# An adaLN, RG-LRU and attention block: its opening rebuilt around a transposed x and four accumulators, and one pair of merge gates moved

## The chip, the cores and the metric

The kernel runs on one core of one Trainium2 chip. The metric is device time in microseconds, the median of three runs. A core has the engines TensorE (PE), VectorE (DVE), ScalarE (ACT), GpSimd (POOL) and SyncE (SP); each runs its own queue of instructions in order and waits on semaphores for the others. SP mostly starts DMAs; here POOL and ACT start some too.

## The reference, cut to what matters

```python
def reference(x, c, positions, ...):          # B=1, S=1024, D=1024
    mod = c @ w_ada + b_ada                    # shift, scale, gate: 3 x 1024
    shift, scale, gate = split(mod, 3)
    h = rmsnorm(x, norm_g) * (1 + scale) + shift
    z = h @ w_in                               # q, k, v, attention gate, RNN x, RNN gate, two merge gates
    ...
    attn = sliding_window_attention_with_sinks(rope(q), rope(k), v, sinks) * silu(ga)
    rnn  = rg_lru(causal_depthwise_conv(xr), ...) * silu(gr)
    m = sigmoid(ma) * (attn @ w_attn_proj) + sigmoid(mr) * (rnn @ w_rnn_proj)
    out = rmsnorm(x + gate * (m @ w_out), final_g)
```

`rmsnorm` multiplies each token of x by 1/sqrt(mean of its squares + eps) and by the gain.

## The kernel before, in words

Everything is float32 in accuracy: every operand of a main product is split into a high part (a rounding to the matmul's own format, called `hh`, `wh`, `nh`) and a low part (what is left: `hl`, `wl`, `nl`), and each product is three matmuls, high by high, weight-low by high, weight-high by low (`mm_k`, L169). A weight half arrives in a tile `r` (`load_half`), ScalarE casts it (`cast`, L101, with a scale L103) and VectorE subtracts (`rest`, L107, with a scale L109) into one of five slots.

The residual stream is used transposed: `xT[kc]` holds 128 of the 1024 features by all 1024 tokens, in eight pieces kc. The **opening** builds it. SP loads x in 8 tiles of 128 tokens (512 KB each). ScalarE and VectorE take turns at the sums of squares, which run along a tile's row (L310, L312); a root, a reciprocal and a scaling follow for each tile (L317 to L319); TensorE transposes 64 blocks (L324) and ScalarE copies them out (L326). The modulation is worked out on VectorE: for each piece two passes `jk` (L221) multiply rows of `w_ada` (SP, 16 loads of 512 KB) with c, broadcast over the partitions by a matmul at L194, and add up each row; `gsc` (L226) and the addition of a bias (L229) finish it. An affine on VectorE (L345) applies it to the piece, ScalarE casts the high halves (L348, `hha` and `hhb` for the first and second 512 tokens of the first four pieces), VectorE subtracts the low halves (L350, `hla`, `hlb`). TensorE accumulates three chunks of 128 output columns over the pieces, the two of k and one of q (48 matmuls of 512 columns each). The framework orders this part; a few `issue_after` push it. The rotary table (positions times frequencies, reduced to a turn by 29 small operations on VectorE, a sine on ScalarE, four DMAs on POOL's queue) is made in its gaps.

From there on **the program is written in the order in which each engine runs it**. The V product (192 matmuls of 256 columns, L1290 to L1292) and the fourth of the opening's chunks (48) follow, while POOL forms differences of the pieces (L382 to L385, `differences`) and ScalarE and VectorE the operands from them (L390, L391). Then come 23 pairs of chunks. A `Pair` computes two chunks with seven half-size products instead of eight: seven slots of 12 matmuls (`product`, L511). Its results stand in four PSUM banks; the pair's place in the list, odd or even (`par`), chooses which of the banks is its second and which its fourth. Work for ScalarE and VectorE is planned into slots: some steps at fixed ones (`at_slot`), others when there is room (`waiting`, `background`), each with a cost. The last pair has an extra step, an addition of its fourth bank to a kept copy (L582).

Of the pairs the last runs beside the attention (scores L1047, their copy L1055, masking L1061, reduction L1066, weights L1071, transposes L1085, values L1119), which goes on while the projections are worked out (`rp`, through `mm_k` at L169). `rp`'s two accumulators are opened when the pairs are done, in the space of the first to fourth banks: the first in `bk[0]` and `bk[1]`, the second in `bk[2]` and `bk[3]`. In the orders below the four banks are called `bk_68` to `bk_71`.

Of the kernel before, what the change touches and what calls it, by code (L numbers as in the profile page):

```python
# [18 lines left out]
ALU = mybir.AluOpType  # L19
# [32 lines left out]
def tile_hybrid_block(ctx, tc, x, pk, rows, posr, posi, invf, c_row, w_ss, w_gate, w_main, w_v,  # L52
# [103 lines left out]
    hx = h_ctx.enter_context(tc.tile_pool(name="hx", bufs=8))  # L156
    xT = [xx.tile([P, S], F32, name=f"xT{kc}") if kc % 4 == 3 else
# [20 lines left out]

    with ExitStack() as st:
        sp = st.enter_context(tc.tile_pool(name="start", bufs=1, side="right"))  # L180
        posr_t = sp.tile([P, 64], I32, name="posr_t")
        dma(posr_t[:], posr)
        invf_t = sp.tile([P, 1], F32, name="invf_t")
        dma(invf_t[:], invf)
        dma(pk_t[:], pk)
        make_identity(nc, ident)

        c_row_t = sp.tile([1, D], F32, tag="xt", name="c_row_t", bufs=10)
        dma(c_row_t[:], c_row)
        one_row = sp.tile([1, P], F32, name="one_row")  # L190
        V.memset(one_row[:], 1.0)
        c_bc = sp.tile([P, D], F32, name="c_bc")
        for hf in range(2):
            T.matmul(bk[hf], one_row[:], c_row_t[:, SL[hf]], start=True, stop=True)  # L194
            A.copy(c_bc[:, SL[hf]], bk[hf])

        xt = []
        starts = []
        wada = {}

        def load_ss(kc):
            for a in range(2):
                wa_t = sp.tile([P, D], F32, tag="xt", name="wada", bufs=10)
                dma(wa_t[:], w_ss[a * D + kc * P:a * D + (kc + 1) * P, :])
                wada[kc, a] = wa_t

        def load_xt(i):
            t = sp.tile([P, D], F32, tag="xt", name="xt", bufs=10)
            dma(t[:], x[i * P:(i + 1) * P, :])
            xt.append(t)  # L210
# [3 lines left out]
        bsc1 = sp.tile([P, 8], F32, name="bsc1")  # L214
        V.tensor_scalar(out=bsc1[:], in0=pk_t[:, PK_BSC:PK_BSC + 8], scalar1=1.0, scalar2=None,
                        op0=ALU.add)

        def modulate(kc):
            for a in range(2):
                jk = sp.tile([P, D], BF16, tag="junk2", name="jk")  # L220
                V.scalar_tensor_tensor(out=jk[:], in0=wada[kc, a][:], scalar=1.0, in1=c_bc[:],  # L221
                                       op0=ALU.mult, op1=ALU.mult,
                                       accum_out=mods[:, a * 8 + kc:a * 8 + kc + 1])
            shf = mods[:, kc:kc + 1]
            g1 = gsc[:, kc:kc + 1]
            V.scalar_tensor_tensor(out=g1, in0=mods[:, 8 + kc:9 + kc],  # L226
                                   scalar=bsc1[:, kc:kc + 1], in1=pcol(PK_NG, kc),
                                   op0=ALU.add, op1=ALU.mult)
            V.tensor_tensor(out=shf, in0=shf, in1=pcol(PK_BSH, kc), op=ALU.add)  # L229
            return g1, shf  # L230

        def load_start(i):
            w = load_w(w_main[i], 0.125 if i == 2 else 1.0)
            starts.append((w, new_ps() if i < 2 else bk[2:]))

        def tiny(name, n=64):
            return sp.tile([P, n], F32, name=name)

        posf = tiny("posf")
        V.tensor_copy(posf[:], posr_t[:])  # L240
        ang = tiny("ang")
        V.tensor_scalar(out=ang[:], in0=posf[:], scalar1=invf_t[:, 0:1], scalar2=None,
                        op0=ALU.mult)
# [55 lines left out]
        for i in range(8):  # L299
            load_xt(i)  # L300
# [1005 lines left out]
    for i in range(4):  # L1306
        differences(i)
# [364 lines left out]
```

## Time and profile before

| | before |
|---|---|
| time, median of 3 runs | 932.31 us (931.2 to 933.3) |
| profiled execution | 934.7 us, of which the span is 933.0 |
| TensorE busy | 907.5 us, 97% of the span |
| VectorE busy | 687.9 us, 74% |
| ScalarE busy | 533.5 us, 57% |
| GpSimd busy | 108.4 us, 12% |
| first main matmul | 27.84 us |

The profile is of one execution. A row of a timeline reads: start, duration, engine, line, operation, output <- inputs, shape, count, and in brackets how long the engine stood idle before it and what ended that. Durations of operations in a row overlap (an engine starts the next before the last has drained), so what one costs is the distance from one start to the next. A row of the windows reads: the stretch and its length, then for each engine the busy time and the number of instructions, TensorE's granted clock, the DMA's share and GB/s. A group's row gives busy time, mean ns of one, and idle time before.

### The profile page before, as it was taken

The numbers are of one execution on the slowest core, as the hardware profiler recorded it, in microseconds if no ns is written. First come the engines' busy times: TensorE is split into PE (matmuls) and PEld (weight loads), VectorE is DVE, ScalarE is ACT, GpSimd is POOL, SyncE is SP. The second block draws the span as 40 slices with busy tenths as digits, with TensorE's granted clock in tenths as the row PEclk, the third lists the DMA queues.
The fourth block names the chain that finished last, engine by engine and source line by source line (L and its number), as shares of the span: only waits on it lengthen the run. The fifth ranks groups of instructions, "written<-read, shape, count | busy, mean of one in ns | idle before, by whom it ended". The sixth has DMA issues, their size and how long they took to land.

```text
span 933.0 us, 12428 instructions
## 1 busy us (share of the span) xinstructions
PE 907.5 (97%) x4261; PEld 752.7 (81%) x4261; DVE 687.9 (74%) x1068; ACT 533.5 (57%) x1040; POOL 108.4 (12%) x161
## 2 busy tenths in 40 slices
PE   5899999999999999999999998999999999999997
PEld 3689888878888888888887887878888888888886
DVE  8977888877669964996677774899999737657422
ACT  7435565454567656775596783888887632213211
POOL 1047000000000000000000001354454300000000
PEclk9999999999999999999999998999999999999999
DMA  8923587951332541354145347997656186436311
GB/s 324 365 69 125 162 285 228 316 191 48 113 105 98 181 158 37 139 172 149 57 147 180 107 163 257 327 328 222 223 177 193 57 309 228 161 123 238 136 68 67
DMA packets 81140, 164.20 MB, mean 176 GB/s; under 512 B 12771, under 2 KB 29155, under 8 KB 81078
## 3 DMA queue, kind: packets, MB, share of 16 engines
q1 hardware_dynamic: 77734, 155.32, 49.0%
q0 software_dynamic: 2192, 6.00, 1.9%
q10 hardware_dynamic: 1152, 2.10, 0.6%
q8 instruction: 33, 0.54, 0.2%
q14 instruction: 29, 0.24, 0.1%
HBM read 114.00 MB, written 49.78 MB: 176 GB/s over the span
## 4 chain that ended last, share of the span: by engine, by line
PE 87%; DVE 5%; DMA 2%; ACT 2%; issue 1%; SPq 1%; POOL 0%; ACTq 0%; DVEq 0%
PE bk L511 44%; PE rp L169 12%; PE pmain L169 8%; PE rp L1537 5%; PE pgate L799 5%; PE pmain L1537 4%; PE s_ps L1047 3%; PE pv L1119 2%; PE pt L1085 1%; PE bk L169 1%; DMA qs<-q_d 1%; DMA r<-w_rp 1%; SPq L59 1%; DVE wl L107 1%; ACT xT L326 1%
## 5 line engine op out<-in xcount | busy, mean ns | idle before, releaser
L511 PE MATMUL bk<-nh,wl 128*128 128x512 f32 x368 | 144.5, 393 | 0.4 <-DVE wl L107 0.4
L511 PE MATMUL bk<-nh,wh 128*128 128x512 f32 x368 | 144.3, 392 | 0.0
L511 PE MATMUL bk<-nl,wh 128*128 128x512 f32 x368 | 144.0, 391 | 0.0
L107 DVE TENSOR_TENSOR wl<-r,wh 128x512 fp32r<-128x512 f32 x108 | 79.4, 739 | 17.8 <-ACT wh L101 17.8
L101 ACT CAST wh<-r 128x512 fp32r<-128x512 f32 x108 | 66.5, 620 | 34.4 <-DMA r<-w_ap 12.2
L511 PEld LDWEIGHTS bk<-nh,wl 128*128 128x128 f32 x368 | 69.7, 189 | 15.8 <-DVE wl L107 1.4
L511 PEld LDWEIGHTS bk<-nl,wh 128*128 128x128 f32 x368 | 69.6, 189 | 14.5
L511 PEld LDWEIGHTS bk<-nh,wh 128*128 128x128 f32 x368 | 69.7, 189 | 14.3
L511 PE MATMUL bk<-hh,wh 128*128 128x512 f32 x184 | 71.6, 389 | 0.0
L511 PE MATMUL bk<-hh,wl 128*128 128x512 f32 x184 | 71.6, 389 | 0.0
L511 PE MATMUL bk<-hl,wh 128*128 128x512 f32 x184 | 71.6, 389 | 0.0
L107 DVE TENSOR_TENSOR wl<-ws,wh 128x512 fp32r<-128x512 f32 x80 | 54.4, 685 | 1.9 <-ACT wh L101 1.9
L59 POOL DMA_DIRECT2D yh_d<-yh x1 | 0.6, 583 | 471.9 <-ACT yh L866 471.9
L1071 ACT ACTIVATE p<-p,small 128x129 f32<-128x129 f32 x128 | 50.1, 401 | 0.0
L101 ACT CAST wh<-ws 128x512 fp32r<-128x512 f32 x80 | 48.0, 614 | 2.0 <-DVE ws L533 1.1
L1047 PE MATMUL s_ps<-ks,qs 128*128 128x256 f32 (+1 forms) x256 | 38.5, 294 | 2.7 <-DMA qs<-q_d 2.5
L511 PEld LDWEIGHTS bk<-hl,wh 128*128 128x128 f32 x184 | 34.5, 188 | 7.2
L511 PEld LDWEIGHTS bk<-hh,wl 128*128 128x128 f32 x184 | 34.5, 188 | 7.1
L511 PEld LDWEIGHTS bk<-hh,wh 128*128 128x128 f32 x184 | 34.5, 188 | 7.0
L1554 ACT ACTIVATE o<-xo 128x1024 f32<-128x1024 f32 (+2 forms) x10 | 8.9, 889 | 52.9 <-DVE xo L1553 52.9
L614 ACT ACTIVATE c<-bk 128x512 f32<-128x512 f32 x31 | 18.5, 598 | 32.7 <-PE bk L511 32.7
L1047 PEld LDWEIGHTS s_ps<-ks,qs 128*128 128x128 f32 x256 | 33.2, 194 | 3.8 <-issue 2.8
(356 smaller groups left out, 2274.3 us busy)
## 6 DMA issues: line engine op xcount, KB each, us to landing
r<-w_main SPq DMA_DIRECT2D x100, 256.0 KB, 4.2
wada<-w_ss SPq DMA_DIRECT2D x16, 512.0 KB, 9.2
qs<-q_d SPq DMA_DIRECT2D x16, 512.0 KB, 6.0
ks<-k_d SPq DMA_DIRECT2D x24, 192.0 KB, 3.8
xt<-x SPq DMA_DIRECT2D x8, 512.0 KB, 5.7
q_d<-rhi SPq DMA_DIRECT2D x16, 256.0 KB, 3.6
q_d<-rlo SPq DMA_DIRECT2D x16, 256.0 KB, 3.0
wg<-w_gate SPq DMA_DIRECT2D x8, 512.0 KB, 5.5
```

What stands on the lines that cost most here:

```text
L59: return eng.dma_start(dst, src)
L101: A.copy(dst[0][:], src)
L107: V.tensor_tensor(out=dst[1][:], in0=src, in1=f32(dst[0][:]), op=ALU.subtract)
L169: mm = T.matmul(ps[hf], ww, xx[kc][hf], start=(kc == 0 and ww is w_h and xx is xh), stop=(kc == KC - 1 and xx is xl))
L326: A.copy(xT[kc][:, SL[hf]], pt)
L511: W["pe"] = T.matmul(ps, ww[:, c], b[kc][xx_], start=(first and kc == 0 and i == 0), stop=(kc == 3 and i == 2), skip_group_check=not first)
L614: A.activation(t["t"], s(), AF.Tanh, scale=0.5)
L799: W["pe"] = T.matmul(ps[:, SL[hf]], ww[:, c0:c0 + P], xx_[:, SL[hf]], start=(ic == 0 and i == 0), stop=(ic == 1 and i == 2))
L1047: W["pe"] = T.matmul(o, qs[:, j, qc], ks[:, b, k0 + (0 if n else P):k0 + 256], start=(b == 0), stop=(b == 1))
L1071: A.activation(px[:, j, :], px[:, j, :], AF.Exp, bias=sm[:, 0, j:j + 1], accum_out=sm[:, 1, j:j + 1])
L1119: W["pe"] = T.matmul(pv[:], b, m[:].rearrange("p j q -> p (j q)"), start=(i == 0), stop=(i == len(prods) - 1))
L1537: T.matmul(ps[:, sl], lhs[k][th][:, ts_], w[:, sl], start=(k == 0 and w is h_ and lhs is mh), stop=(k == KC - 1 and lhs is ml))
```

## The change

It rebuilds the opening and moves the first pair of merge gates.

- x also comes in transposed (`x_t`), and is loaded straight into `xT`, eight loads at the head of SP's queue. The transposes, their copies and the scaling of tiles are gone (x itself is still read at the end of the kernel).
- The sums of squares now run over partitions: ScalarE squares each piece (L254) into one of four buffers (`acc`, `sqa`, `r_bc`, `sqb`), VectorE adds pieces 0+1, 2+3 and 4+5 (L256), and TensorE sums with 40 matmuls of one moving column (L250), the squares being the weights, into one bank. VectorE reduces (L339, L340), ScalarE takes the root, VectorE the reciprocal (L346), and TensorE spreads the result over the partitions with 8 matmuls (L348). VectorE multiplies the pieces by it (L353 from PSUM, L356 from a copy).
- The modulation rows get their bias as a 1025th column, so two small operations per piece go. ScalarE makes the high halves directly from the normed piece with scale and bias (L359), and applies the affine to the piece (L363).
- The whole opening is in a written order. The angle operations stand first on VectorE; the positions and frequencies are loaded on POOL's queue, c and the constants on ScalarE's.
- Four chunks are accumulated over the pieces, the two of k and both of q. Their first halves of weights have tiles of their own (`first`), the second halves are cast and subtracted at pieces 2 and 3. At pieces 3 to 7 the chunks go in the order 3, 2, 0, 1.
- The differences move from POOL to VectorE (L468 to L471), between the two halves of the V product.
- `MA[0]`, the first pair of merge gates, leaves the list of pairs (23 become 22). Its two chunks are computed as plain products of 48 matmuls (`merge`), one behind the other, directly behind V, with their tanh and stores.
- `gate_row` (the last modulation row, worked out in the background) starts ahead of `v_prep`, in a third waiting list; RNN steps that need its pool wait for it.

The diff, cut to its core:

```diff
-        for kc in range(KC):
-            pt = bk[kc % (2 if hf else 4)]
-            for j in range(4):
-                T.transpose(pt[:, j * P:(j + 1) * P],
-                            xt[hf * 4 + j][:, kc * P:(kc + 1) * P], ident[:])
-            A.copy(xT[kc][:, SL[hf]], pt)
...
+        dma(c_row_t, c_row, A)
+        dma(pk_t[:], pk, A)
+        dma(posr_t[:], posr, G)
+        dma(invf_t[:], invf, G)
...
+        for kc in range(KC):
+            dma(xT[kc][:], x_t[kc * P:(kc + 1) * P, :])
+        load_ss(0)
+        for i in range(4):
+            load_wh(i, 0)
...
+        def sums(i, kc, js=range(8)):
+            for j in js:
+                T.matmul(bk[2][:, 8 * i + j:8 * i + j + 1], sqs[kc % 4][:, j * P:(j + 1) * P],
+                         one[:, 0:1], start=True, stop=True)
+
+        def square(kc):
+            A.activation(sqs[kc % 4][:], xT[kc][:], AF.Square)
+            if kc < 6 and kc % 2:
+                V.tensor_tensor(out=sqs[kc % 4 - 1][:], in0=sqs[kc % 4 - 1][:],
+                                in1=sqs[kc % 4][:], op=ALU.add)
+                sums(kc // 2, kc - 1)
...
+        def spread(hf):
+            r1 = rr[:, 4 * hf:4 * hf + 4]
+            V.reciprocal(r1, r1)
+            for j in range(4):
+                T.matmul(bk[hf][:, j * P:(j + 1) * P], r1[:, j:j + 1].to_broadcast([P, P]),
+                         ident[:], start=True, stop=True)
...
+        def high(kc, hf):
+            A.activation(hh[kc][hf], xT[kc][:, SL[hf]], AF.Identity,
+                         scale=gsc[:, kc:kc + 1], bias=mods[:, kc:kc + 1])
...
+        angles()
+        square(0)
+        square(1)
+        for kc in range(2, 6):
+            square(kc)
+        square(6)
+        sums(3, 6)
+        square(7)
+        for hf in range(2):
+            sums(4, 7, range(4 * hf, 4 * hf + 4))
+        modulate(0, 0)
+        root_of(0)
+        root_of(1)
+        spread(0)
+        spread(1)
...
+        for kc in range(1, KC):
+            norm(kc)
+            for hf in range(2):
+                high(kc, hf)
+            affine(kc)
+            if kc == 1:
+                table()
+            if kc + 1 < KC:
+                for a in range(2):
+                    modulate(kc + 1, a)
+            if kc in (2, 3):
+                for i in (0, 1) if kc == 2 else (2, 3):
+                    cast_w(i, 1)
+                    rest_w(i, 1)
+            low(kc)
...
+            if kc < 3:
+                for terms in ("h", "l"):
+                    for w, ps in starts:
+                        mm_k(ps, w, kc, terms=terms)
+            else:
+                for i in (3, 2, 0, 1):
+                    w, ps = starts[i]
+                    mm_k(ps, w, kc)
...
-    pairs = [Q[1], MA[0], Q[2], MA[1], Q[3], XR[0], GR[0], GA[0], XR[1], GR[1], GA[1], GR[2],
-             XR[2], GA[2], GA[3], GR[3], XR[3], MA[2], MA[3]] + MR
+    pairs = [Q[1], Q[2], MA[1], Q[3], XR[0], GR[0], GA[0], XR[1], GR[1], GA[1], GR[2], XR[2], GA[2],
+             GA[3], GR[3], XR[3], MA[2], MA[3]] + MR
...
+    merge(0, bk[:2])
+    v_store(bk[2:], 1)
...
+    merge(1, bk[2:])
+    merge_out(1, bk[2:])
```

Three places of the new order, each beside the old one. First TensorE at the start of the program, in before from the last transposes to the first main matmuls (`pmain` and `bk_70` are accumulators, `hha_158` the high first half of piece 0):

```order
L324 MATMUL bk_68<-ident,xt 128x128 x3
L324 MATMUL bk_69<-ident,xt 128x128 x3
L324 MATMUL bk_68<-ident,xt 128x128
L324 MATMUL bk_69<-ident,xt 128x128
L324 MATMUL bk_68<-ident,xt 128x128 x4
L324 MATMUL bk_69<-ident,xt 128x128 x4
```

and in the changed kernel from its first instruction to the first main matmuls (`one` is a column of ones, `rr` the reciprocal roots):

```order
L228 MATMUL bk_68<-sqb,one 128x512
L228 MATMUL bk_69<-sqb,one 128x512
L250 MATMUL bk_70<-one,acc 128x1 x8
L250 MATMUL bk_70<-one,r_bc 128x1 x8
L250 MATMUL bk_70<-one,acc 128x1 x8
L250 MATMUL bk_70<-one,r_bc 128x1 x8
L250 MATMUL bk_70<-one,sqb 128x1 x8
L348 MATMUL bk_68<-ident,rr 128x128 x4
L348 MATMUL bk_69<-ident,rr 128x128 x4
L170 MATMUL pmain<-hha_158,wh_203 128x512
```

Transposes gave way to sums and spreading matmuls, in one fixed order. Next VectorE at piece 3, before (`xT_191` is the piece, `hla_172` and `hlb_173` its low halves):

```order
L345 TENSOR_SCALAR xT_191<-xT_191,gsc,mods 128x1024
L221 SCALAR_TENSOR_TENSOR jk,mods<-wada,c_bc 128x1024
L350 TENSOR_TENSOR hla_172<-xT_191,hha_170 128x512
L221 SCALAR_TENSOR_TENSOR jk,mods<-wada,c_bc 128x1024
L350 TENSOR_TENSOR hlb_173<-xT_191,hhb_171 128x512
L229 TENSOR_TENSOR mods<-mods,pk_t 128x1
```

and now (the piece is `xT_193`):

```order
L356 TENSOR_TENSOR xT_193<-xT_193,r_bc 128x1024
L237 SCALAR_TENSOR_TENSOR jk,mods<-wada,c_bc 128x1025 [waits DMAHW2_49]
L237 SCALAR_TENSOR_TENSOR jk,mods<-wada,c_bc 128x1025 [waits DMAHW3_49,DVE_49]
L241 SCALAR_TENSOR_TENSOR gsc<-mods,pk_t 128x1 [waits DVE_49]
L109 SCALAR_TENSOR_TENSOR wl<-r,wh 128x512 [waits DMAHW0_49,Activation_49]
L109 SCALAR_TENSOR_TENSOR wl<-r,wh 128x512 [waits DMAHW1_49,Activation_49]
L368 TENSOR_TENSOR hla_172<-xT_193,hha_170 128x512
L368 TENSOR_TENSOR hlb_173<-xT_193,hhb_171 128x512
```

The low halves of the piece now stand behind both modulation passes of the next piece and two weight subtractions. Last TensorE where the pairs end and `rp` begins, before:

```order
L511 MATMUL bk_70<-nl,wh 128x512
L1119 MATMUL pv<-phc,vs 128x512 [waits DMASW5_49,DVE_49,Activation_49]
L1119 MATMUL pv<-plc,vs 128x512 [waits DVE_49]
L1119 MATMUL pv<-phm,dv 128x512 [waits DMASW4_49,Pool_49]
L1119 MATMUL pv<-plm,dv 128x512 [waits Pool_49]
L1085 MATMUL pt<-ident,p 128x128 [waits PE_49]
L1085 MATMUL pt<-ident,p 128x128 x3
L1047 MATMUL s_ps<-ks,qs 128x256 [waits DMAHW1_49,DMAHW2_49,DMAHW0_49,DVE_49]
L1047 MATMUL s_ps<-ks,qs 128x256 x7
L169 MATMUL rp_5620<-hha_158,wh 128x512 [waits Activation_49]
```

and now:

```order
L597 MATMUL bk_69<-nl,wh 128x512
L1212 MATMUL pv<-phc,vs 128x512 [waits DMASW7_49,DVE_49,Activation_49]
L1212 MATMUL pv<-plc,vs 128x512 [waits DVE_49]
L1212 MATMUL pv<-phm,dv 128x512 [waits DMASW6_49,Pool_49]
L1212 MATMUL pv<-plm,dv 128x512 [waits Pool_49]
L1178 MATMUL pt<-ident,p 128x128 [waits PE_49]
L1178 MATMUL pt<-ident,p 128x128 x3
L1140 MATMUL s_ps<-ks,qs 128x256 [waits DMAHW6_49,DMAHW7_49,DMAHW0_49,DVE_49]
L1140 MATMUL s_ps<-ks,qs 128x256 x7
L170 MATMUL rp_5538<-hha_158,wh 128x512 [waits DVE_49]
```

The last product writes the second bank (`bk_69`) instead of the third (`bk_70`), and the first matmul of `rp` waits for VectorE instead of ScalarE: for the last pair's addition of that bank (L582 before, L668 now).

More of the change, by code (lines that the diff above doesn't have):

```diff
@@ L51, in tile_hybrid_block @@
 @with_exitstack
-def tile_hybrid_block(ctx, tc, x, pk, rows, posr, posi, invf, c_row, w_ss, w_gate, w_main, w_v,
+def tile_hybrid_block(ctx, tc, x, x_t, pk, rows, posr, posi, invf, c_row, w_ss, w_gate, w_main, w_v,
                       w_g, w_ap, w_rp, w_out, out):
@@ L918, in out_row @@
             dma(gate_d, t["row"])
+            W["gate"] = True
         def spare(base):
@@ L949, in lam_1 @@
             V.memset(pcol(PK_NG, 0), 1.0)
-        waiting[0].extend([slots(4), [("S", 0, 0, start)], slots(3)])
+        waiting[2].extend([slots(4), [("S", 0, 0, start)], slots(3)])
         todo = [[("A", 1.5, 0, lam_a)], [("D", 0, 1.0, lam_0)]]
```

423 lines of the change are left out of this document (219 added, 204 removed).

## The prediction

> **What bounds the kernel now.** I read the page first: the span, the busy shares, and the chain that ended last.
>
> ```profile
> span 933.0 us, 12428 instructions
> PE 907.5 (97%) x4261; PEld 752.7 (81%) x4261; DVE 687.9 (74%) x1068; ACT 533.5 (57%) x1040; POOL 108.4 (12%) x161
> PE 87%; DVE 5%; DMA 2%; ACT 2%; issue 1%; SPq 1%; POOL 0%; ACTq 0%; DVEq 0%
> ```
>
> TensorE is busy 97% of the span and carries 87% of the last chain. So two things can move the time: the number of matmuls, and the stretches in which TensorE waits. The profiled execution took 934.7 us, 1.7 more than its span, against a median of 932.3; I work out a difference on the span and add it to the median. The table of windows shows where it waits: in the opening.
>
> ```profile
> core 0: us, PE busy (x) PEld busy (x) DVE busy (x) ACT busy (x) POOL busy (x), PEclk, DMA share, GB/s
> 10.00:20.00 10.00, 6.46 (x27) 5.12 (x28) 9.47 (x30) 9.47 (x22) 2.05 (x3) 1.00 1.03 395
> 30.00:40.00 10.00, 8.86 (x38) 6.63 (x38) 10.00 (x22) 2.28 (x4) 0.00 (x0) 1.00 1.03 398
> 40.00:50.00 10.00, 8.57 (x37) 6.66 (x36) 10.00 (x21) 3.84 (x7) 0.00 (x0) 1.00 0.59 229
> 200.00:300.00 100.00, 100.00 (x443) 82.75 (x442) 71.11 (x95) 57.36 (x84) 0.00 (x0) 1.00 0.35 118
> ```
>
> From 200 to 300 us 443 matmuls run in 100 us, so a 512-column matmul costs 0.226 us (0.227 below). From 30 to 50 us VectorE is busy all the time and TensorE is not: VectorE sets the pace there. TensorE's timeline dates the opening.
>
> ```profile
> 3.82 3.75 PE L194 MATMUL bk<-c_row_t,one_row 1*128 1x512 f32 x4 [3.82 <-DMA c_row_t<-c_row]
> 16.59 5.16 PE L324 MATMUL bk<-ident,xt 128*128 128x128 f32 x28 [1.27 <-DVE xt L319]
> 27.84 0.74 PE L169 MATMUL pmain<-hha,wh 128*128 128x512 f32 x2
> 33.35 0.73 PE L169 MATMUL pmain<-hha,wh 128*128 128x512 f32 x2 [1.09 <-ACT hha L348]
> 47.04 0.38 PE L1290 MATMUL bk<-wh,hha 128*128 128x256 f32 x1 [0.78 <-ACT wh L101]
> 48.08 0.73 PE L169 MATMUL pmain<-hh,wh 128*128 128x512 f32 x2 [0.65 <-ACT hh L348]
> 87.70 0.28 PE L1291 MATMUL pmain<-wl,hh 128*128 128x256 f32 x1
> 87.82 0.28 PE L1292 MATMUL pmain<-wh,hl 128*128 128x256 f32 x1
> 87.94 0.40 PE L169 MATMUL pmain<-hha,wh 128*128 128x512 f32 x1
> ```
>
> The first main matmul starts at 27.84. Between it and 87.94 lie 144 of 512 columns and the 192 of the V product, 0.12 apart: 32.7 + 23.0 = 55.7 us of work in 60.1, so 4.4 are lost to waits. The 48 of the fourth chunk follow without a wait (10.9), so **before has done these 384 matmuls at 98.8 us**. The new opening does the same 384, only the order differs; this is the mark to compare with.
>
> **Part 1, the start of the main matmuls.** Gone are 64 transposes, their copies and the scaling of x. In their place stands one chain, each link waiting for the one before:
>
> ```profile
> cs_d<-csn POOLq DMA_DIRECT2D x3, 32.0 KB, 5.2
> posr_t<-posr SPq DMA_DIRECT2D x1, 32.0 KB, 1.8
> 6.51 0.23 DVE L283 TENSOR_TENSOR tt<-fa,sb 128x64 f32<-128x64 f32 x1
> 6.77 0.20 DVE L248 TENSOR_SCALAR rt<-tt 128x64 f32<-128x64 f32 x1
> 7.00 0.23 DVE L254 TENSOR_TENSOR ft<-tt,rt 128x64 f32<-128x64 f32 x1
> 6.28 1.06 ACT L310 ACTIVATE junk<-xt 128x1024 bf16<-128x1024 f32 x1 [4.19 <-DMA xt<-x]
> 16.70:18.70 2.00, 1.97 (x9) 1.56 (x10) 0.00 (x0) 1.59 (x4) 1.00 1.01 384
> 20.30:21.40 1.10, 1.10 (x13) 1.10 (x12) 0.00 (x0) 1.10 (x3) 1.00 1.01 384
> ```
>
> The positions (32 KB) move from SP's queue, where they landed in 1.8 us, to POOL's, where 32 KB took 5.2: from an issue near 1.3 they are there at about 6.7, with the frequencies behind them. All 29 angle operations now stand first on VectorE, nearly each waiting for the last: 0.22 to 0.26 apart by the three rows, 6.4 together, to 13.1. Behind them is queued the first pair add of the squares (1.2, to 14.3), for which the sums wait. The squares are done by then: x now leads SP's queue and lands whole at about 13 (8 loads of 0.52 MB at 395 GB/s, from 2.6 at the latest), its first pieces far earlier; the 2.1 MB behind it (the first modulation rows and four half chunks of weights) follow by 18.5, ahead of their use. POOL issues nothing else there, and c_row and the constants go out on ScalarE's queue, which is idle then.
>
> Each of the 40 sums is a matmul with one moving column whose 128x128 weights are fresh. No row shows one. The c_row matmuls (two instructions, four records) say that an fp32 matmul runs as two records; the transposes say what a record with fresh 128x128 fp32 weights costs: 0.22 in the window from 16.70, 0.11 (counting rows cut at both edges) in that from 20.30, after 3.5 us of unbroken work, though the granted clock reads 1.00 in both. So a sum costs 0.22 to 0.43.
>
> The rest of the chain: sums of the first pair (8), two squares that reuse their buffers (ScalarE waits for those sums; 2 x 1.03), the third pair's add (1.2), the last 24 sums, the root and reciprocal (1.1 with hand-offs, as four small operations), four spreading matmuls of two records each (0.9 to 1.7), then the first half's norm can start. With the first 8 sums slow and the rest fast: 14.3 + 3.4 + 2.1 + 1.2 + 5.3 + 1.1 + 0.9 = **28.3**. All fast gives 26.7, all slow 34.1. The first main matmul comes one norm and one ScalarE pass later, near 29.5, against 27.84.
>
> The Trainium skill ("TensorE: Matmul & The Clock Gate", "Part 1: The HAM clock gate") says that TensorE runs at half rate by default and at full rate only after about 3.4 us of sustained work. By that rule this change, whose sums come in bursts with waits between, does them slowly where the transposes of before ended fast. The trace agrees on the ramp (0.22, then 0.11 after 3.5 us), not in its clock column. It is the second rival below.
>
> **Part 2, the loop over the eight pieces of x.** Four accumulators instead of three: 24 matmuls a piece, 5.4 us, so TensorE has more to do per piece of VectorE's work. But up to piece 3 VectorE has the weights of all four chunks to finish too.
>
> ```profile
> 45.80 1.23 DVE L221 SCALAR_TENSOR_TENSOR jk<-wada,c_bc 128x1024 bf16<-128x1024 f32 x1
> 46.94 0.17 DVE L229 TENSOR_TENSOR mods<-mods,pk_t 128x1 f32<-128x1 f32 x1
> 47.02 0.70 DVE L109 SCALAR_TENSOR_TENSOR wl<-r,wh 128x512 fp32r<-128x512 f32 x1
> 47.62 0.70 DVE L107 TENSOR_TENSOR wl<-r,wh 128x512 fp32r<-128x512 f32 x1
> 48.22 0.23 DVE L226 SCALAR_TENSOR_TENSOR gsc<-mods,bsc,pk_t 128x1 f32<-128x1 f32 x1
> 48.35 1.23 DVE L221 SCALAR_TENSOR_TENSOR jk<-wada,c_bc 128x1024 bf16<-128x1024 f32 x1
> ```
>
> From start to start, a 128x1024 pass takes 1.14, a 128x512 pass 0.60, a gsc 0.13. From the first norm to the low half of piece 3, VectorE has 2 half norms and 3 whole ones (4.6), 8 modulations with 4 gsc (9.6), 8 low parts of weights (4.8) and 8 of x (4.8): 23.8. I add 1.0 for turns in which it waits for ScalarE between norm and low half (bounds 0 and 2); the affine is ScalarE's now and not in this sum. So piece 3 is complete at 28.3 + 24.8 = 53.1. TensorE has then caught up: it holds four matmuls of piece 3 and stops, with 116 of the 192 left, 26.3 us, beside which VectorE needs 4.7 a piece and keeps ahead. The 192 end at 79.4. The V weights can be cast only when slots come free, as before: 0.9 of wait (0.78 in the row at 47.04). V then ends at 79.4 + 0.9 + 23.0 = 103.3, against 98.8: **+4.5**.
>
> **Part 3, the merge gates.** One pair (7 slots of 12 matmuls, 84) leaves the list, two plain chunks (2 x 48) come in behind V: 12 x 0.227 = **+2.7**, on TensorE, with no bounds to speak of. Their tanh and stores lie beside matmuls; so do the differences, which leave POOL (they cost VectorE 16 x 0.60 = 9.6, beside 23 of V product and 22 of merge gates); if that cover failed, what they delay is the operands of the first pair. The chunk's second weights and the gate row's move have the same cover.
>
> **Part 4, the end of the pairs.** With 22 pairs instead of 23 the parity of the last one flips. Its last product goes to the second bank instead of the third; and the first accumulator of the projection behind it, opened in the space of the first two banks, can then only start when VectorE has added that bank up. Before, it waited for an early ScalarE copy.
>
> ```profile
> 599.28 1.20 PE L1047 MATMUL s_ps<-ks,qs 128*128 128x256 f32 x8
> 600.77 0.73 PE L169 MATMUL rp<-hha,wh 128*128 128x512 f32 x2 [0.29 <-ACT u L560]
> 602.52 0.59 ACT L1055 COPY p<-s_ps 128x512 f32<-128x512 f32 x1
> 603.62 0.74 DVE L1061 COPY_PREDICATED p<-mgt,s_ps 128x512 f32<-128x512 uint32 x1
> 604.46 0.69 DVE L1066 TENSOR_REDUCE small<-p 128x4 f32<-128x516 f32 x1
> 605.07 0.68 DVE L582 TENSOR_TENSOR u<-u,bk 128x512 f32<-128x512 f32 x1
> ```
>
> Here the add ended at 605.75, 5.0 after the projection started, and nobody waited. On VectorE it stands behind the masking and the reduction of the scores that TensorE issues just ahead. In the new kernel TensorE would stand from the end of these scores (about 600.5) through the copy, the masking, the reduction and the add: 0.59 + 0.84 + 0.61 + 0.68 and hand-offs, 3.2 if nothing is queued ahead of the copy, up to 5.0 as in this trace. Less than 2.7 isn't possible unless the scores come earlier. I take 3.5, less the 0.3 that before waits there: **+3.2**.
>
> **The sum:** 4.5 + 2.7 + 3.2 = 10.4 on the span, so 932.3 + 10.4 = **942.7**.
>
> **The rivals.** *The sums cost little* (15%): all fast, 26.7 in place of 28.3, gives 941.1. For it speaks that TensorE has just run c_row's matmuls; against it, nearly 7 us without work (7.6 to 14.3) before the first sum. The Trainium skill ("TensorE: Matmul & The Clock Gate", "LDWEIGHTS (loading the stationary operand)") puts a load of 128 columns at P/1.2 ns, 107 ns, and names no rate for it; the window from 20.30 agrees, that from 16.70 doesn't.
>
> *The sums stay slow* (20%): each burst is too short, the norm starts at 34.1, and the time is 948.5. For it: the transposes in the window from 16.70, behind shorter bursts and a wait of 1.27, still ran slowly. Against it: those of the last bursts, at 20.30, did not, and 24 sums in a row are 5 us or more.
>
> *The last add does not hold the projection* (9%): scores far ahead of it, or an early add; 942.7 - 3.2 = 939.5.
>
> *Faster* (5%): the chain keeps up with x itself. x is whole at about 13, so square, sums, root and spread put the first norm at 18 to 19 at best, if the angles don't hold the adds and the sums run under the loads. Then the norm comes 9.3 earlier and the whole to 933.4; to pass 930.4 by itself it would need the norm at 16.0, before the transfers allow it. So its point is a norm at 19 together with a last add that holds nothing up: 933.4 - 3.2 = 930.2, faster. Against it stand POOL's slow queue and the angles in front.
>
> Left for the forecast: 51%. A measurement of this kernel can tell about 0.2%, 1.9 us. Faster by more: 0.05; within: 0.03 (the cheap start without the last wait, or the early start alone); slower: 0.92. The range goes from 936.5 (fast sums, VectorE never waiting for ScalarE and no wait for the last add: 942.7 - 1.6 - 1.0 - 3.2 = 936.9, rounded down) to 949.5 (slow sums, 948.5, and a second microsecond of VectorE's waits).
>
> **What would show it.** Right: the first main matmul at 28 to 31; VectorE without a gap to piece 3 and TensorE waiting for the low half of piece 3 (`xT` by way of L368) by 2 to 4 us; V done near 103; 12 more matmuls of 512 columns; `rp` waiting for the add at L668 for about 3. Wrong: main matmuls from 20 or so, no wait in the loop, or `rp` starting straight behind the scores. Main matmuls from 34 would show the slow sums.

## The result, and the profile after

The changed kernel takes 961.13 us (median of 4 runs, 960.87 to 961.55) against 932.66 (4 runs, 931.2 to 933.3): a ratio of 1.031, 95% interval 1.029 to 1.033. It is slower, as forecast, but by 28 us instead of 10, outside the range. The first lines of its page:

```profile
span 959.2 us, 12443 instructions
PE 924.6 (96%) x4305; PEld 769.6 (80%) x4305; DVE 684.2 (71%) x1044; ACT 535.1 (56%) x1019; POOL 86.5 (9%) x148
PE 90%; DVE 4%; DMA 2%; ACT 2%; issue 1%; POOL 0%; SPq 0%; DVEq 0%; ACTq 0%; POOLq 0%
```

TensorE is *busier* than before (924.6 us against 907.5), and that is the first hint: 12 matmuls of 512 columns explain 2.7 of these 17 us. TensorE's timeline shows the rest.

```profile
17.09 3.58 PE L250 MATMUL bk<-one,acc 128*128 128x1 f32 x16 [10.03 <-DVE acc L256]
...
30.86 3.55 PE L250 MATMUL bk<-one,sqb 128*128 128x1 f32 x16
35.43 3.75 PE L348 MATMUL bk<-ident,rr 128*128 128x128 f32 x16 [1.01 <-DVE rr L346]
39.10 0.79 PE L170 MATMUL pmain<-hha,wh 128*128 128x512 f32 x1
43.54 0.63 PE L170 MATMUL pmain<-hhb,wl 128*128 128x512 f32 x1
44.73 0.40 PE L170 MATMUL pmain<-hlb,wh 128*128 128x512 f32 x1
61.54 0.39 PE L170 MATMUL bk<-hhb,wl 128*128 128x512 f32 x1
64.69 0.79 PE L170 MATMUL bk<-hla,wh 128*128 128x512 f32 x1 [2.76 <-DVE hla L368]
66.32 0.63 PE L170 MATMUL bk<-hhb,wh 128*128 128x512 f32 x1
117.03 0.40 PE L170 MATMUL bk<-hha,wh 128*128 128x512 f32 x1
```

Read the counts: the 40 sums are 80 records, two each, and 16 of them take 3.4 us from start to start, 0.213 a record, from the first at 17.09 to the last at 34.3. They never get faster, though TensorE works without a gap for 17 us. The spreading matmuls are slow too, and so are the main ones up to 43.96: 0.63 long at 43.54, where a main matmul at full rate is 0.40 long (44.73). Main matmuls start at 39.10 (27.84 before). Behind the matmul of 61.54 TensorE stops for the low half of piece 3, 2.76 us, and runs slow for 3.3 us after it. The V product is done at 117.03, where the kernel before has done as many matmuls at 98.8: 18.2 later. The head of the chain is on VectorE:

```profile
6.39 0.20 DVE L265 CAST posf<-posr_t 128x64 f32<-128x64 int32 x1 [5.31 <-DMA posr_t<-posr]
9.22 0.26 DVE L267 TENSOR_SCALAR ang<-posf,invf_t 128x64 f32<-128x64 f32 x1 [2.64 <-DMA invf_t<-invf]
15.82 1.22 DVE L256 TENSOR_TENSOR acc<-acc,sqa 128x1024 f32<-128x1024 f32 x1
37.52 0.69 DVE L353 TENSOR_TENSOR xT<-xT,bk 128x512 f32<-128x512 f32 x1 [0.63 <-PE bk L348]
64.56 0.69 DVE L368 TENSOR_TENSOR hlb<-xT,hhb 128x512 fp32r<-128x512 f32 x1
```

The frequencies, second in GpSimd's queue, arrive at 9.2; the angles run to 15.8; only then comes the first pair add, and the first sum. At the end of the pairs stand these rows, of ScalarE, VectorE and TensorE:

```profile
619.78 1.20 PE L1140 MATMUL s_ps<-ks,qs 128*128 128x256 f32 x8
622.29 0.59 ACT L1148 COPY p<-s_ps 128x512 f32<-128x512 f32 x1
623.39 0.73 DVE L1154 COPY_PREDICATED p<-mgt,s_ps 128x512 f32<-128x512 uint32 x1
624.83 0.68 DVE L668 TENSOR_TENSOR u<-u,bk 128x512 f32<-128x512 f32 x1
625.57 1.22 PE L170 MATMUL rp<-hha,wh 128*128 128x512 f32 x2 [4.59 <-DVE u L668]
630.86 0.56 PE L1212 MATMUL pv<-phc,vs 128*128 128x512 f32 x1
```

The projection waits 4.59 us for the add, and its first 12 matmuls take 5.3 us, 0.43 each, instead of 2.7. So of the 26.2 us that the span grew, 18.2 are there when V is done, 2.7 are the 12 matmuls, 6.9 belong to the projection's start (4.6 of pause and 2.6 of slow matmuls, less the 0.3 that it waited before), and the 1.6 that this is too much come back elsewhere; the waits listed for TensorE do not show where.

The windows tell how to read the clock column:

```profile
17.09:34.40 17.31, 17.31 (x80) 17.22 (x80) 3.45 (x4) 4.00 (x4) 0.00 (x0) 1.00 0.58 224
64.69:68.00 3.31, 3.31 (x7) 2.44 (x8) 3.27 (x5) 1.56 (x3) 0.00 (x0) 0.50 0.74 277
625.57:630.86 5.29, 5.29 (x13) 4.13 (x14) 0.72 (x2) 0.60 (x1) 0.00 (x0) 0.50 0.38 144
```

The slow stretches at 64.7 and 625.6 have a granted clock of 0.50. The sums have 1.00 and are just as slow: in these traces the column shows 1.00 up to the first change of state in a run, whatever the rate is, and only the distance between matmuls tells it.

### The profile page after: what moved, and what is told of

Read it like the earlier page. It is cut to its first block, busy times and chain, and to the rows that moved or that the text cites. A ratio compares the mean times of both kernels' runs of the same rounds, so it can differ in the third digit from the quotient of the medians.

```text
span 959.2 us, 12443 instructions
## 1 busy us (share of the span) xinstructions
PE 924.6 (96%) x4305; PEld 769.6 (80%) x4305; DVE 684.2 (71%) x1044; ACT 535.1 (56%) x1019; POOL 86.5 (9%) x148
## 4 chain that ended last, share of the span: by engine, by line
PE 90%; DVE 4%; DMA 2%; ACT 2%; issue 1%; POOL 0%; SPq 0%; DVEq 0%; ACTq 0%; POOLq 0%
PE bk L597 41%; PE rp L170 14%; PE pmain L170 6%; PE rp L1633 5%; PE pgate L891 5%; PE pmain L1633 4%; PE bk L170 4%; PE s_ps L1140 3%; PE pv L1212 3%; PE bk L250 2%; PE pt L1178 1%; DMA qs<-q_d 1%; PE bk L1383 1%; PE bk L1384 1%; PE bk L1385 1%
## 5 line engine op out<-in xcount | busy, mean ns | idle before, releaser
L597 PE MATMUL bk<-nh,wl 128*128 128x512 f32 x352 | 138.0, 392 | 0.4 <-DVE wl L107 0.4
L597 PE MATMUL bk<-nh,wh 128*128 128x512 f32 x352 | 137.8, 392 | 0.0
L597 PE MATMUL bk<-nl,wh 128*128 128x512 f32 x352 | 137.6, 391 | 0.0
L597 PEld LDWEIGHTS bk<-nh,wl 128*128 128x128 f32 x352 | 66.5, 189 | 15.2 <-DVE wl L107 1.4
L597 PEld LDWEIGHTS bk<-nh,wh 128*128 128x128 f32 x352 | 66.4, 189 | 13.9
L597 PEld LDWEIGHTS bk<-nl,wh 128*128 128x128 f32 x352 | 66.5, 189 | 13.7
L597 PE MATMUL bk<-hh,wh 128*128 128x512 f32 x176 | 68.6, 390 | 0.0
L597 PE MATMUL bk<-hh,wl 128*128 128x512 f32 x176 | 68.6, 390 | 0.0
L597 PE MATMUL bk<-hl,wh 128*128 128x512 f32 x176 | 68.5, 389 | 0.0
L107 DVE TENSOR_TENSOR wl<-ws,wh 128x512 fp32r<-128x512 f32 x76 | 51.8, 686 | 0.5 <-ACT wh L101 0.5
L700 ACT ACTIVATE c<-bk 128x512 f32<-128x512 f32 x29 | 17.3, 597 | 31.0 <-PE bk L597 31.0
```

The costliest lines, as they stand in the source:

```text
L107: V.tensor_tensor(out=dst[1][:], in0=src, in1=f32(dst[0][:]), op=ALU.subtract)
L597: W["pe"] = T.matmul(ps, ww[:, c], b[kc][xx_], start=(first and kc == 0 and i == 0), stop=(kc == 3 and i == 2), skip_group_check=not first)
L700: A.activation(t["t"], s(), AF.Tanh, scale=0.5)
```

## The experiments

Theory after the result: (a) TensorE's clock stays at half for as long as the array itself works little, and one-column sums with fresh weights are little work; (b) the opening is one chain, so what is late at its head is late at its end; (c) behind it VectorE paces TensorE up to piece 3; (d) the pause at the projection is the bank that the flipped parity hands to the last pair. Rivals stand with each run. Times are compared with runs of the kernel before on the same chip in the same session: 931.95, 931.99, 930.82 and 931.29 for the four sessions. The changed kernel was timed once, beside 932.66, so a difference to its 961.13 is uncertain by up to 1.8 us for the session alone.

**e1: the angles behind the adds.**

```diff
-        angles()
         square(0)
...
         modulate(0, 0)
+        angles()
         root_of(0)
```

> The 29 angle operations stand behind the three pair adds on VectorE, everything else as changed; the loads on GpSimd's queue stay. Theory (the opening is one chain, and what is late at its head is late at its end): the first sum starts when the first pair add can, 10.8 us (the second square ended at 9.6 there, plus 1.2) instead of 17.1; the sums still take 17.1, the first norm comes at 31.2 instead of 37.5, and the whole kernel is 6.3 us faster, about 954.8. Rival (the loop behind it is bound by the modulation rows' loads or by VectorE's total work, and an earlier start is eaten up): less than 3 us gained, TensorE waiting longer in the loop.

Measured: 955.86, ratio 1.0262 (1.0244 to 1.028), span 952.9. TensorE's rows:

```profile
9.92 3.57 PE L250 MATMUL bk<-one,acc 128*128 128x1 f32 x16 [3.84 <-DVE acc L256]
28.27 3.75 PE L348 MATMUL bk<-ident,rr 128*128 128x128 f32 x16 [1.01 <-DVE rr L346]
110.18 0.40 PE L170 MATMUL bk<-hha,wh 128*128 128x512 f32 x1
```

The first sum comes 7.2 earlier, V's end 6.85 earlier, the span of the profiled run is 6.3 shorter, and the medians differ by 5.3: (b) holds, most of it is passed on, and nothing in the loop up to V eats it. The angles and GpSimd's queue in front of the first add cost 5 to 7 us.

**e2: wide work ahead of the sums.**

```diff
+        for _ in range(10):
+            T.matmul(bk[3], one[:], c_bc[:, SL[0]], start=True, stop=True)
+
         mods = sp.tile([P, 16], F32, name="mods")
```

> Ten fp32 matmuls of 512 columns with no use are put ahead of the sums, so that TensorE works without a gap from 8 us to the first sum at 17. Theory A (TensorE runs at half rate until wide work releases it, and one-column matmuls don't count as such work): the sums begin at 0.107 us a record, as the fast transposes did, and fall back to 0.213 after some 3 to 7 us; the first main matmul comes 1.5 to 4 us earlier, and the main matmuls start slow as before. Theory B (a record with one column costs 0.213 in itself, the clock has nothing to do with it): 0.213 from the first to the last sum, first main matmul at 39. Theory C (released once, it stays released while TensorE is busy): 0.107 for all 80 records, 8.5 us gained.

Measured: 958.18 (one run), span 956.5.

```profile
5.99 10.82 PE L233 MATMUL bk<-c_bc,one 128*128 128x512 f32 x20
16.65 1.84 PE L253 MATMUL bk<-one,acc 128*128 128x1 f32 x16
18.35 1.93 PE L253 MATMUL bk<-one,r_bc 128*128 128x1 f32 x16
21.84 3.57 PE L253 MATMUL bk<-one,acc 128*128 128x1 f32 x16 [1.57 <-DVE acc L259]
```

Its windows over the second and third of these bursts and on:

```profile
18.35:20.20 1.85, 1.85 (x18) 1.84 (x17) 0.00 (x0) 1.68 (x2) 0.00 (x0) 1.00 1.05 421
21.84:32.20 10.36, 10.36 (x48) 10.32 (x48) 1.09 (x2) 0.58 (x1) 0.00 (x0) 0.50 0.45 179
```

This tells the three theories apart: the same instructions take 0.106 a record right behind the wide work, and 0.213 from 21.84 on, with the clock now shown at 0.50. The record has no price of its own (B falls). The fall itself lies across a wait of 1.57 us, so this run does not tell which of the two, the narrow work or the wait, brought it. But before's transposes stayed fast across a wait of 1.63; of the two rows, the first has eight slow ones and the second eight fast ones, behind that wait:

```profile
13.32 2.00 PE L324 MATMUL bk<-ident,xt 128*128 128x128 f32 x8 [1.63 <-DVE xt L319]
23.38 1.15 PE L324 MATMUL bk<-ident,xt 128*128 128x128 f32 x8 [1.63 <-ACT xT L326]
```

And 48 records on end do not bring the clock back: to be busy is not enough (C falls), and of theory A the part on the sums stands. The main matmuls start 2.2 earlier, and not slow, as A had it: from 38.98 on they are 0.23 apart (see e9).

**e3: the projection's accumulators exchanged.**

```diff
-        rp_acc.extend(psr.tile([P, S], F32, name=f"rp{i}") for i in range(2))
+        rp_acc.extend([psr.tile([P, S], F32, name=f"rp{i}") for i in range(2)][::-1])
```

> The two accumulators of the projection change places, so that the first stands in the third and fourth banks, and the last pair's addition reads a bank of the second. Theory: the 4.6 us pause ahead of the first projection matmul and the 11 half-rate matmuls behind it (0.2 each) go, 6.5 to 7.3 us gained, about 954. Rival (the pause only moves: another reader of these banks, or the second accumulator four matmuls later, holds TensorE): less than 3 us gained.

Measured: 955.67 (951.48 to 957.34), ratio 1.0254 (1.0225 to 1.0282). The row of the projection has no wait and no slow matmuls:

```profile
623.40 0.73 PE L170 MATMUL rp<-hha,wh 128*128 128x512 f32 x2
```

The pause is gone and has not moved. The gain, 5.5 by the medians, is a little under what was expected; in its profiled run V ends 0.9 later than in the changed kernel's, and the attention has 0.8 more of small waits.

**e4: the same exchange in the kernel before.** The same line is edited in before.

> The same exchange of places in the kernel before, where the last pair's fourth bank is the third: now the first accumulator of the projection lies in it. Nothing else is changed. Theory: the pause appears there too, TensorE waits for the addition that ended at 605.75 (5.0 us after the projection started) and runs slow for some 10 matmuls after it: 6 to 7 us slower, about 939. Rival (the pause belongs to the new order of the work, not to the banks): no change, 932.5.

Measured: 939.3, ratio 1.0085 (1.0064 to 1.0106), 7.3 slower.

```profile
603.44 1.22 PE L169 MATMUL rp<-hha,wh 128*128 128x512 f32 x2 [4.58 <-DVE u L582]
```

The old order with the bank at the wrong place shows the same pause (4.58) and the same slow matmuls behind it. With e3 that settles (d).

**e5: ones as the weights.**

```diff
-            for j in js:
-                T.matmul(bk[2][:, 8 * i + j:8 * i + j + 1], sqs[kc % 4][:, j * P:(j + 1) * P],
-                         one[:, 0:1], start=True, stop=True)
+            for hf in range(2):
+                T.matmul(bk[hf], one[:], sqs[kc % 4][:, SL[hf]], start=i == 0, stop=i == 4)
...
+            V.tensor_scalar(out=r_bc[:, SL[hf]], in0=bk[hf], scalar1=1.0 / D, scalar2=EPS,
+                            op0=ALU.mult, op1=ALU.add)
+            A.activation(r_bc[:, SL[hf]], r_bc[:, SL[hf]], AF.Sqrt)
+        for hf in range(2):
+            V.reciprocal(r_bc[:, SL[hf]], r_bc[:, SL[hf]])
```

> The operands of the sums change sides: 128x128 ones are the weights and the squares the moving side, 512 columns at a time, fp32, 10 matmuls accumulating in two banks. Every partition gets the sum at once, so the 8 spreading matmuls go, and the root and reciprocal run over 128x512 from the banks. The angles stay in front. Theory (wide fp32 work releases TensorE's clock after some 3.5 us, one-column work never does): 20 records, the first 4 or 5 at 0.85 us and the rest at 0.43, sums from 17.1 to about 28; root and reciprocal 3 us, first norm about 31 instead of 37.5, main matmuls at 0.23 from their first: 7 to 9 us faster, 952 to 954. Rival (TensorE is slow in the first 40 us whatever it does): 0.85 throughout, sums end at 34 as now, no gain.

Measured: 960.26, ratio 1.031 (1.0282 to 1.0339): no gain, a miss. TensorE's rows and one of VectorE:

```profile
16.71 3.78 PE L250 MATMUL bk<-acc,one 128*128 128x512 f32 x4 [9.73 <-DVE acc L255]
25.66 1.88 PE L250 MATMUL bk<-r_bc,one 128*128 128x512 f32 x4
39.25 0.79 PE L170 MATMUL pmain<-hha,wh 128*128 128x512 f32 x1 [9.99 <-ACT hha L358]
29.91 6.55 DVE L398 RECIPROCAL r_bc<-r_bc 128x512 f32<-128x512 f32 x2
```

The clock does what (a) says: four records at 0.85, then 0.43 from 21 us on, sums done at 29 instead of 34.4. What I had priced too low is the reciprocal: root and reciprocal were put at 3 us together, and the reciprocal alone takes 3.3 for 128x512, five times another pass of that shape, and is needed twice. It eats the gain, and TensorE, idle for 10 us beside it, starts the main matmuls slow again.

**e6: the merge gates back in the list.** The pair `MA[0]` returns to `pairs`, and `merge` and `merge_out` go.

> The first pair of merge gates goes back into the list (23 pairs) and the two plain merge products behind V are gone; everything else as changed. Rival (the move is a pure cost: 12 matmuls and the flipped parity): 2.7 + 6.8 = 9.5 us gained, about 951.5. Theory (the 96 matmuls behind V also cover VectorE, which has the differences, the ropes of k and the pairs' operands to do before the pairs can run): the pause at the projection goes (6.8) and 12 matmuls (2.7), but TensorE stops behind V, at 117, until the operands are made, which in the changed kernel took to 143.5: 10 to 15 us of new waits, 961 to 967.

Measured: 966.57, ratio 1.0373 (1.0326 to 1.042), some 5 slower than the changed kernel; with two runs only, the two intervals touch (1.0326 against 1.033).

```profile
PE bk L597 <- ACT wh L103: 10.3, 1, 10.3
PE bk L597 <- DVE wl L109: 3.1, 1, 3.1
```

Behind V TensorE now waits 13.4 us for the first pair's weights, and runs slow after it (0.43 from matmul to matmul). The wait at the projection is gone, as the parity is back. So the 96 plain matmuls are no pure cost: with the differences on VectorE they are the cover that the pairs' preparation needs. Their price of 2.7 buys that.

**e7 and e8: three and four repairs.** Sums with ones as weights in one pass (the squares rounded to the matmul's own format), positions and frequencies first on SP, the accumulators exchanged; e8 also moves four subtractions:

```diff
                 for i in (0, 1) if kc == 2 else (2, 3):
                     cast_w(i, 1)
-                    rest_w(i, 1)
             low(kc)
+            if kc in (3, 4):
+                for i in (3, 2) if kc == 3 else (0, 1):
+                    rest_w(i, 1)
```

> Three repairs together: ones as weights of the sums (the squares rounded to the matmul's own format, one pass, in place of exact fp32 sums), positions and frequencies loaded first on SP's queue, the projection's accumulators exchanged. Theory: angles done by 10, x whole at 14, sums of 10 matmuls at 0.23 to 0.43 end about 16 to 17, first norm at 20 to 21 instead of 37.5, low half of piece 3 about 27 us later (as measured in the changed kernel), 192 matmuls done by 75, V by 98: 18 to 19 gained there and 6.8 at the projection, 934 to 937. It does not pass the kernel before, by the 12 extra matmuls (2.7). Rival (VectorE's loop is bound by the arrival of the modulation rows): low half of piece 3 no earlier than about 55, 940 or more.

> As the one with three repairs, and the four subtractions of the second weight halves move behind the low half of pieces 3 and 4, where they are first needed. Theory (VectorE paces TensorE up to the low half of piece 3): it comes 2.4 us earlier, of which 1 to 2.4 remain; 932 to 935. Rival (VectorE only gets behind one piece later): no change against three repairs.

Measured: 947.56, ratio 1.0174 (1.0141 to 1.0207), and 944.21, ratio 1.0134 (1.0106 to 1.0162). e7 misses its number (first norm at 30.4 instead of 21) for the reason of e5, the same reciprocals, 22.7 to 29.2, and for a second one: VectorE's adds wait twice for ScalarE's squares, 2.07 us each, and the sums end at 21 to 22 instead of 17. In the waits of TensorE from 30 to 95 us, first e7's, then e8's row for piece 3:

```profile
PE bk L170 <- DVE hla L375: 2.8, 1, 2.8
```

```profile
PE bk L170 <- DVE hla L375: 0.3, 1, 0.3
```

With four passes of 0.6 moved past the low half, the wait falls from 2.8 to 0.3 and 3.4 us are gained: (c) holds, VectorE paces TensorE there.

**e9 to e11: more columns for the sums.** 64 moving columns instead of one; e10 adds the repairs of SP's queue, the accumulators and the subtractions, e11 also four wide matmuls ahead. In these three the five groups are gathered in one bank in a way that doesn't give the reference's sum; the instructions and their order are as described, and only times are read.

```diff
-                T.matmul(bk[2][:, 8 * i + j:8 * i + j + 1], sqs[kc % 4][:, j * P:(j + 1) * P],
-                         one[:, 0:1], start=True, stop=True)
+                T.matmul(bk[2][:, 64 * j:64 * j + 64], sqs[kc % 4][:, j * P:(j + 1) * P],
+                         one[:, 0:64], start=i == 0, stop=i == 4, skip_group_check=True)
```

> One edit against the changed kernel: each of the 40 sums has 64 moving columns of ones instead of one, into its own 64 columns of the bank, accumulated over the five groups; the squares stay the weights, and the root reads one column in 64. Nothing is computed that the sums need, TensorE's array only works longer beside each weight load. Theory (what keeps the clock down is how little the array works, not the number of instructions): slow for 3.5 to 7 us, then fast; sums from 17 to 26 to 28 instead of 34.4, spreading and main matmuls fast from their start, 7 to 10 us faster, 951 to 954. Rival (64 columns are still too little, as the first 20 transposes with 128 might suggest): no gain, 961, or slower by the longer records.

> The 64 columns, and with them: positions and frequencies first on SP's queue, the projection's accumulators exchanged, the second weight halves' subtractions behind the low halves of pieces 3 and 4. Theory: first sum at 11.3, the third pair's squares wait for the first eight sums, last sum at about 23.5, first norm at 25 to 26 (30.5 in the run with four repairs, which lost 6.5 to the wide reciprocals), main matmuls fast at once (2.8 more): 7 to 8 below that run, 936 to 938. Rival (the loop behind is bound by loads): no better than 942.

> As the one before, with four fp32 matmuls of 512 columns without use ahead of the sums, so that they begin fast. Theory: 16 sums at 0.22 instead of 0.43 and squares 4 and 5 let go earlier, first norm at 23 to 24, 2 below the run before it: 934 to 936. It does not reach the kernel before (932.0), because the 12 extra matmuls (2.7) stay and the loop's pace is VectorE's. Rival (the sums then wait for x's transfers, which land last at 14 to 15): no change against the run before it.

Measured: 958.34 (ratio 1.0301, 1.0283 to 1.032), 946.79 (1.0167, 1.015 to 1.0183), 947.16 (1.0178, 1.0158 to 1.0198). The last burst of e9's sums, and three rows of e11:

```profile
30.40 3.62 PE L250 MATMUL bk<-one,sqb 128*128 128x64 f32 x16
```

```profile
6.00 5.29 PE L233 MATMUL bk<-c_bc,one 128*128 128x512 f32 x8
11.44 2.00 PE L253 MATMUL bk<-one,acc 128*128 128x64 f32 x16 [0.15 <-DVE acc L259]
16.79 3.68 PE L253 MATMUL bk<-one,acc 128*128 128x64 f32 x16 [1.56 <-DVE acc L259]
```

64 columns beside a fresh 128x128 weight load are still too little: 0.21 to 0.22 a record to the last sum, 17 us on end, and by the ratios e9 is no faster than the changed kernel, the rival's case. e10 and e11 miss their numbers by that; e11's sums start fast and fall back as e2's did. (e11's V ends 1.6 earlier than e10's; TensorE loses that again later, to a longer wait for a DMA, 3.7 against 2.6, and to 2.2 of waits for `wo`.)

Behind these sums e9 shows something else:

```profile
34.81 3.53 PE L347 MATMUL bk<-ident,rr 128*128 128x128 f32 x16 [0.79 <-DVE rr L345]
40.54 0.39 PE L170 MATMUL pmain<-hhb,wl 128*128 128x512 f32 x1
```

The spreading matmuls have fresh weights too, but 128 columns, and by their end the clock is released: the main matmuls are at full rate, as in e2, e3 and e10. In the changed kernel, e1, e6, e11 and e12 the same 16 records did not do it. The opening of e3 is the changed kernel's to the instruction, so this differs from one execution to the next; what decides it is open. In the time it makes no difference, since VectorE paces this part: TensorE waits 2.77 for the low half of piece 3 in e9, 2.76 in the changed kernel.

**e12: eight sums.** VectorE, idle beside the sums, adds all eight squared pieces; 8 sums of one column are left; eleven wide matmuls ahead, and the three repairs of e10.

```diff
+            sq = sqs[1 + (kc - 1) % 3 if kc else 0]
+            A.activation(sq[:], xT[kc][:], AF.Square)
+            if kc:
+                V.tensor_tensor(out=acc[:], in0=acc[:], in1=sq[:], op=ALU.add)
```

> The cause put to use: VectorE, which stood idle beside the sums, adds all eight squared pieces into one (7 adds instead of 3), so that 8 one-column sums are left of 40; eleven fp32 matmuls of 512 columns without use keep TensorE at work from 6 us until then; and the three other repairs (positions and frequencies first on SP's queue, the projection's accumulators exchanged, the second weight halves' subtractions later). The result is the reference's. Theory: adds end at 18.2, 8 sums at 0.21 end at 20, root and spread, first norm at 22 to 23, main matmuls fast from their first, VectorE's loop as before (23.7 to the low half of piece 3), V done at 97 to 99 where the kernel before is at 98.8 by the same count; the rest is 12 matmuls (2.7): 933 to 936. Rival (TensorE's clock falls back in the 2 us of root and hand-offs, or x comes later than thought): first norm at 25 or later, 937 to 940.

Measured: 938.94 (937.48 to 940.38), ratio 1.008 (1.0064 to 1.0097), 22 us below the changed kernel and 7.6 above the one before.

```profile
6.24 11.27 PE L233 MATMUL bk<-c_bc,one 128*128 128x512 f32 x22
19.61 3.55 PE L253 MATMUL bk<-one,acc 128*128 128x1 f32 x16 [2.09 <-DVE acc L260]
23.95 3.75 PE L348 MATMUL bk<-ident,rr 128*128 128x128 f32 x16 [0.80 <-DVE rr L346]
27.62 0.79 PE L170 MATMUL pmain<-hha,wh 128*128 128x512 f32 x1
```

The sums fall from 17.3 us to 3.4. The wide matmuls end 2.1 us before the sums, and did nothing for them: 0.213 again. The first norm comes at 26.0, the rival's case, and the time is the rival's. Main matmuls start at 27.62, where before had 27.84, and V ends at 102.9 against 98.8: what is left against before is these 4.1 and the 12 matmuls (2.7), 6.8 of the 7.6. The slow start of the main matmuls is no part of it: from the first norm to the first matmul with piece 3's low half e12 takes 23.8 us, and e10, whose main matmuls start fast, 23.6. That is VectorE's loop. No run beats the kernel before.

## Why the prediction was wrong, point by point

- **Direction and the four terms: right.** All four are there at the places named: the late chain, the wait for the low half of piece 3, 12 matmuls, the wait for the last add. The sum was 10.4; the span grew by 26.2. V came 13.7 later than forecast (117.03, not 103.3), and the next three points hold 13.4 of that: 6.4, 2.8 and 4.2.
- **"With the first 8 sums slow and the rest fast": the step that failed.** All 40 ran at 0.427 each. I took from the transposes (0.22, then 0.11 after 3.5 us of unbroken work) that unbroken work releases the clock. It is not being busy that counts: sums of 1 and of 64 columns beside a fresh weight load never released it (e2, e9), while the transposes have 128. That the array's work is what counts fits all of these, but is argued: no run changes it alone. The stretch of sums took 17.3 us instead of 12.0, the root and spread 3.1 instead of 2.0. My second rival had the rate but the wrong reason ("each burst is too short"): the bursts ran on end, and long ones are as slow. Its first norm at 34.1, with the 2.8 of the next point, is 36.9 of the 37.5 measured. Slow sums alone were forecast at 948.5, so this is the largest of the errors and not all of them.
- **The head of the chain: undersized by 2.8.** The first sum came at 17.1, not 14.3: the frequencies needed 7 us from issue on GpSimd's queue, not 5.2. With the angles out of the way, 5 to 7 us come back (e1).
- **The loop: undersized by 2.8 + 1.4.** From the first norm to the end of piece 3's low half VectorE took 27.6, not 24.8; I left out the accumulator reads behind each modulation pass (about 0.12, eight times) and put its waits at 1.0, when they came to 2.6 (2.2 for ScalarE, over the bound of 2, and 0.4 for the second spreading). And TensorE's own pause there, 2.8, was followed by half-rate matmuls (1.4), which I had not priced. The pace itself was right (e8).
- **Merge gates: right**, 2.7; e6 shows that their cover, which I named in passing, is worth more than they cost.
- **The last add: right place, 3.2 instead of 6.9.** The pause was 4.6, within the bounds (2.7 to 5.0), but I took the lower part; and the 12 half-rate matmuls behind it (2.6) were not in the sum, though before's own pause at 569.9 showed such a stretch.
- **The range** ended at 949.5, since I let its upper end be slow sums alone and did not add the clock's price at the two pauses. A pause of more than 2 us ahead of wide matmuls had a second price behind it in these traces, 1.4 us (piece 3) and 2.6 us (projection) in the changed kernel.

## What to carry to other kernels

When matmuls are traded for others, count not only how many records there are but how much the array works in them: here a long stream of narrow ones with fresh weights ran at half rate to its end, and in some runs the wide ones behind it began so too. Leave narrow sums to an engine that is idle beside them: in e12 four more adds on VectorE replace 32 of the 40 sums, and the first norm comes 6.0 earlier than in e10, which has the same other repairs. And when an item leaves a list in which places alternate, look at which bank the last one now gets, and who opens it next.

## What the runs showed of the hardware

- A matmul record with a fresh 128x128 fp32 weight load takes 0.21 to 0.22 us at half rate and 0.106 to 0.114 at full, with 1 and with 64 moving columns much alike; streams of them for 17 us did not release the clock (after, e9), and where wide work had released it, it was lost among them (e2, e11: fast for some 3.5 us, then, behind a wait of 1.6, slow for 10 on end). 512 columns released it within 3.5 to 4.2 us (e5), 128 beside a fresh load in before's transposes and by the end of the spreading, or just behind it, in e2, e3, e9 and e10 (3.4 to 4 us), but not in the 3.7 us of spreading of after, e1, e6, e11 and e12. In the streams that stayed slow to their end, the sums, the moving side was ones; in those that released the clock it was data or the identity. Whether the columns or these values decide was not tested apart. The Trainium skill ("TensorE: Matmul & The Clock Gate", "Part 1: The HAM clock gate") speaks of about 3.4 us of sustained activity and says that the number of matmuls does not matter; the first agrees with e5, but by these runs activity is not the same as an engine that is never idle.
- The granted clock reads 1.00 until the first change in a run, also where every matmul is at half rate; later slow stretches read 0.50 (after, e2, e12).
- A reciprocal of 128x512 on VectorE takes 3.3 us (e5, e7), where a subtraction of that shape takes 0.6 from start to start.
- A transfer of 0.5 KB, second on GpSimd's queue, landed 7 us after its issue at 2.0, under x's loads (after).
